# Split-weight buffers handed out block by block, and three of four block sums on VectorE instead of two

## The chip, the cores and the metric

The kernel runs on one core of one Trainium2 chip. The metric is the device time of one execution in microseconds (us); less is better. Times before come from three runs and one profiled execution.

## The reference, cut to what matters

One step of a streaming encoder with two layers for 640 rows (512 of a prompt, 8 x 16 of running streams), in fp32. Layer 0 is a convolution module, layer 1 an attention over a shared K and V; each is followed by a feed-forward network (FFN), and only these two networks are touched here:

```python
D_MODEL = 1024
FFN_HIDDEN = -(-8 * D_MODEL // (3 * 256)) * 256      # 2816

def swiglu_ffn(h, g, w_in, w_out):
    a, b = jnp.split(rms_norm(h, g) @ w_in, 2, axis=-1)
    return h + (jax.nn.silu(a) * b) @ w_out
...
    for l in range(DEPTH):
        ...
        h = swiglu_ffn(h, norm_ffn[l], w_ffn_in[l], w_ffn_out[l])
    return rms_norm(h, norm_final), jnp.stack(new_hist, axis=0), k, v
```

## The kernel before, in words

**Order of the program.** The convolution module runs first (to about 250 us of the span), then `ffn(0, ...)` (to about 690 us), the attention (to about 1060 us), `ffn(1, ...)` (to about 1505 us) and the last norm. Instructions are put in order at build time by a scheduler that runs a model of the engines' times; code under `tc.high_priority(offset=HP)` goes ahead of other code that is ready. On the chip each engine's queue then runs in that fixed order.

**A product in three passes.** A weight and an activation are each split into a rounded upper part (`hi`) and a rest (`lo`), and a product is hi x hi + lo x hi + hi x lo: three matmuls for each 128 rows of the contraction (`product`, line 374). The split of a weight is `put` (line 318): ScalarE (ACT) copies the source to `hi`, VectorE (DVE) subtracts it for `lo`. `cut` (line 322) does this for some columns of a pair of tiles.

**Seven products in place of eight.** The 640 columns of activations are two halves of 320 (`NH`), and the rows of the hidden layer are taken in pairs of 128. Most 2 x 2 products of blocks are formed with seven block products (a Strassen-like scheme): of a weight block with the quarters a11, a12, a21, a22 it needs a11, a12 and a22, and four sums. `w_seven` (line 352) loads a raw block (four quarters of 512 columns for `w_in`, 384 for `w_os`), forms the sums and cuts all seven. In order of the code:

- the SyncE (SP) queue loads a21 into `s1` and the whole block into `raw`;
- GpSimd (POOL) issues two adding DMAs from memory: a22 is added to `s1` (line 361), a11 to the quarter a21 of `raw` (line 362);
- one wide cut of a12 and a11 together (line 363), then DVE adds `s1` to a11 (line 364), and the cuts of that sum (XT2) and of `s1` (XT1);
- the cuts XT3 (of a21 + a11), XT4 (of a22) and X22 (of a12 plus the large sum, added by DVE on line 370).

The large pair `whi`, `wlo` (2048 columns, two buffers, `wbig`) takes the first four, the ring `shi`, `slo` (512 columns, three buffers, `wring`) the last three. `raw` has two buffers and `s1` two.

**Who uses a block when.** `seven` (line 460) runs the products of a `w_in` block in the order X11, X21, XT2, XT1, XT3, and hands the last two, XT4 and X22, to the next block, which runs them behind its own X11 and X21. A product of a `w_in` block has 12 matmuls, of a `w_os` block 9. For the output weights the order is written out in the string `QORD`: of each two characters the first names the product (5 is XT1, 1 X11, 2 X21, 6 XT2, 3 X22, 7 XT3, 4 XT4) and the second the pair of output rows; `a0` and `a1` are the products left over from the last `seven`.

**Counts.** A layer has three `w_in` blocks that go the plain way (`w_std`, eight products each), 19 that go through `w_seven`, and 12 of `w_os` (three chunks of four): 38 + 24 = 62 blocks of seven for both layers. The last four rows of hidden blocks go through plain products whose weights are split into `wbig` pairs at the end (line 602).

Of the kernel before, what the change touches and what calls it, by code (L numbers as in the profile page):

```python
# [9 lines left out]
F32R = mybir.dt.float32r  # L10
# [5 lines left out]
P = 128  # L16
# [41 lines left out]
X11, X21, XT2, XT1, XT3, XT4, X22 = range(7)  # L58
NCH, CW = 3, 6
HIX = {X11: 0, X21: 1, XT1: 2, XT2: 3, XT3: 4, X22: 5, XT4: 6}  # L60
QORD = "50 a0 10 a1 20 51 11 21 60 30 61 70 31 52 40 71 12 22 41 62 32 53 72 13 23 42 63 33"
BO = "a0 s0 a1 s1 b0 b1 t0 p0 c0 t1 c1"
BL = "a0 s0 a1 s1 t0 b0 b1 c0 t1 c1 p0"
SSQ1 = 'ppapappp'
# [10 lines left out]
def tile_trunk(ctx, tc, xT, vecs, hist, w_pw1, w_pw2, w_in0, w_out0, w_os0, w_in1, w_out1, w_os1,  # L75
               w_kq, w_v, w_o, rel, kc, vc, y_out, convp_out, convs_out, k_out, v_out):
    nc = tc.nc

    cst = ctx.enter_context(tc.tile_pool(name="cst", bufs=1))
    wp = ctx.enter_context(tc.tile_pool(name="wp", bufs=2))  # L80
# [11 lines left out]
    def nm(s):  # L92
        uid[0] += 1
        return f"{s}_{uid[0]}"
# [191 lines left out]
    def ffn(l, w_in, w_out, w_os, tail, hf):  # L286
        nonlocal w2, mm, tp

        def fpool(name, bufs, **kw):
            return hf.enter_context(tc.tile_pool(name=f"{name}{l}", bufs=bufs, reuse_waits="tile",  # L290
                                                 **kw))
# [13 lines left out]
        wx = fpool("wx", 2)  # L305
# [4 lines left out]
        sub, add, mult = ALU.subtract, ALU.add, ALU.mult  # L310

        def two(i, dt=F32R):
            return hpf.tile([P, 2, NH], dt, tag=f"d{i}", name=nm("hid"))
# [4 lines left out]
        def put(hi, lo, src):  # L318
            nc.scalar.activation(out=hi, in_=src, func=AF.Copy)  # L319
            nc.vector.tensor_tensor(out=lo, in0=src, in1=hi.bitcast(F32), op=sub)  # L320

        def cut(w, o, src):
            c = slice(o, o + src.shape[-1])
            put(w[0][:, c], w[1][:, c], src)

        def wraw():
            return wp.tile([P, 2048], F32, tag="raw", name=nm("raw"))

        def wbig():
            return [wp.tile([P, 2048], F32R, tag="w" + t, name=nm("w" + t)) for t in ("hi", "lo")]  # L330

        def wring():
            return [wx.tile([P, 512], F32R, tag="s" + x, name=nm("s" + x), bufs=3)
                    for x in ("hi", "lo")]

        def w_std(src, small):
            raw = wraw()
            if small:
                ws = [(wring(), 0) for _ in range(3)]
                ws.append(([two(i).rearrange("p a n -> p (a n)") for i in (12, 13)], 0))  # L340
            else:
                w = wbig()
                ws = [(w, 512 * i) for i in range(4)]
            for i in range(0, 2048, 1024):
                nc.sync.dma_start(raw[:, i:i + 1024], src[:, i:i + 1024])
                with tc.high_priority(offset=HP):
                    n = 512 if small else 1024
                    for j in range(i, i + 1024, n):
                        cut(*ws[j // 512], raw[:, j:j + n])
            return ws[1], ws[0], ws[2], ws[3]  # L350

        def w_seven(src, out=False):
            n = src.shape[-1] // 4
            raw, w = wraw(), wbig()
            s1 = wx.tile([P, 512], F32, tag="s1", name=nm("s1"))[:, :n]
            nc.sync.dma_start(s1, src[:, 2 * n:3 * n])
            nc.sync.dma_start(raw[:, :4 * n], src)
            a12, a11, a21, a22 = (raw[:, n * i:n * i + n] for i in range(4))
            ws = {X11: (w, n), X21: (w, 0), XT2: (w, 2 * n), XT1: (w, 3 * n)}
            with tc.high_priority(offset=HP):  # L360
                nc.gpsimd.dma_start(s1, src[:, 3 * n:4 * n], accum_op=add)
                nc.gpsimd.dma_start(a21, src[:, n:2 * n], accum_op=add)
                cut(w, 0, raw[:, :2 * n])
                nc.vector.tensor_tensor(out=a11, in0=s1, in1=a11, op=add)  # L364
                cut(w, 2 * n, a11)
                cut(w, 3 * n, s1)
                for x in (X22, XT3, XT4) if out else (XT3, XT4, X22):
                    ws[x] = (wring(), 0)
                    if x == X22:
                        nc.vector.tensor_tensor(out=a12, in0=a12, in1=a11, op=add)  # L370
                    cut(*ws[x], {X22: a12, XT3: a21, XT4: a22}[x])
            return ws

        def product(pt, w, xs, first, o=0):
# [85 lines left out]
        def seven(src, sink, before):  # L460
            ws = w_seven(src)
            pa, pb = mmt()[:, :NH], mmt()[:, :NH]
            xproduct(pa, ws[X11], X11, True)
            t1 = keep("t1", pa)
            before(0)
            xproduct(pb, ws[X21], X21, True)
            plus(t1, pb)
            silu(t1, t1)
            before(1)
            xproduct(pa, ws[XT2], XT2, False)  # L470
            t2 = keep("t2", pa)
            pe = mmt()[:, :NH]
            xproduct(pe, ws[XT1], XT1, True)
            xproduct(pa, ws[XT3], XT3, False)
            t3 = keep("t3", pa)
            plus(t3, pe)

            def after(i):
                if i == 0:
                    xproduct(pa, ws[XT4], XT4, False)  # L480
                    sink(0, t1, pa)
                else:
                    xproduct(pe, ws[X22], X22, False)
                    plus(t2, pe)
                    silu(t2, t2)
                    sink(1, t2, t3)

            return after

        def out_chunk(c, HH, HL, after):  # L490
            ws, pts = {}, {}
            prod = {5: ("e", XT1, True, 1, 1), 1: ("a", X11, True, 0, 0),
                    2: ("b", X21, True, 0, 0), 6: ("a", XT2, False, 1, 0),
                    3: ("e", X22, False, 1, 0), 7: ("a", XT3, False, 1, 1),
                    4: ("a", XT4, False, 0, 1)}

            def go(i, u):
                if u not in ws:
                    o = (4 * c + u) * 12 * P
                    ws[u] = w_seven(w_os[:, o:o + 12 * P], True)  # L500
                b, x, first, half, row = prod[i]
                if first:
                    pts[b, u] = mmt()[:, :NH]
                pt = pts[b, u]
                product(pt, ws[u][x], list(zip(HH[x], HL[x])), first)
                hv = h[:, 2 * u + row, half * NH:half * NH + NH]
                with tc.high_priority(offset=HP):
                    nc.vector.tensor_tensor(out=hv, in0=hv, in1=pt, op=sub if row else add)  # L508

            for t in QORD.split():  # L510
                if t[0] == "a":
                    after(int(t[1]))
                else:
                    go(int(t[0]), int(t[1]))
            return lambda i: go((7, 4)[i], 3)
# [42 lines left out]
        for jj in range(NSTD):  # L558
            wstd.append(w_std(w_in[jj], jj == 0))
            std(wstd[jj], 0, sinks[jj])  # L560
            if jj == 0:
                with tc.high_priority(offset=HP):
                    stats(1)
                    xnorm(x12, 1, 0)
                    xput(XT4, x12)
                    xnorm(x22, 1, 4)
                    xput(X22, x22)
# [32 lines left out]
        after(1)  # L600
        done = []
        for m0 in (0, 4):
            raw, w = wraw(), wbig()
            nc.sync.dma_start(raw.rearrange("p (m c) -> p m c", m=4),
                              w_out[m0:m0 + 4].rearrange("m p c -> p m c"))
            with tc.high_priority(offset=HP):
                for o in range(0, 2048, 1024):
                    cut(w, o, raw[:, o:o + 1024])
            done += [(m0 + i, [(w[0][:, b:b + P], w[1][:, b:b + P])
                               for b in range(512 * i, 512 * i + 512, P)]) for i in range(4)]  # L610
        for g0, n in tail:
            for m, w in done:
# [3 lines left out]
                with tc.high_priority(offset=HP):  # L616
                    nc.vector.tensor_tensor(out=h[:, m, g0:g0 + n], in0=pt[:, :n],
                                            in1=h[:, m, g0:g0 + n], op=add)
# [243 lines left out]
    early.close()  # L862
    hf = ExitStack()
    ffn(0, w_in0, w_out0, w_os0, GR, hf)
    hf.close()
    gr[:] = GR
# [286 lines left out]
    for p in range(NP):  # L1153
# [8 lines left out]
        for op in (BL if p == NP - 1 else BO).split():  # L1162
            i = int(op[1])
# [20 lines left out]
    for g0, n in ((0, NH), (NH, NH)):  # L1184
        for m in range(KT):
# [3 lines left out]
                            for wh, wl in wos for k in range(2)],  # L1189
                [(oT[4 + k][0][:, g0:g0 + n], oT[4 + k][1][:, g0:g0 + n]) for k in range(4)])  # L1190
            nc.vector.tensor_tensor(out=h[:, m, g0:g0 + n], in0=pt[:, :n], in1=h[:, m, g0:g0 + n],
                                    op=ALU.add)
    at.close()
    early.close()

    hf = ExitStack()
    ffn(1, w_in1, w_out1, w_os1, ((256, 384), (0, 256)), hf)
    tw[0] = 384
    sqt[:] = "sq", "acc", 1
# [8 lines left out]
    for g in (1, 0):  # L1208
        g0, n = GR[g]
        for k in range(KT):  # L1210
            if k < FP[g]:
                nc.vector.scalar_tensor_tensor(out=hp(g, k), in0=hp(g, k), scalar=col(V_NFIN, k),
                                               in1=bcs[g], op0=ALU.mult, op1=ALU.mult)
# [100 lines left out]
```

## Time and profile before

| | |
|---|---|
| time, median of three runs | 1539.4 us (1534.5 to 3146.81) |
| time of the profiled execution | 1537.75 us |
| its span | 1535.9 us |
| mean granted TensorE clock | 0.983 |
| busy: TensorE (PE) / its weight loads (PEld) | 95% / 90% |
| busy: DVE / ACT / POOL | 70% / 48% / 22% |
| from HBM, written | 193.82 MB, 11.61 MB |

Busy shares are of the span. A matmul is shown with its whole length, and consecutive ones overlap. In rows of groups stand the line of the kernel, engine, operation, output from inputs, shape and count, then the busy time, the mean of one in ns, and the engine's idle time just before with what ended it. In rows of waits stand the total in us, the count and the longest. Rows of instructions begin with start and length in us; in brackets is the engine's idle time before it.

### The profile page before, as it was taken

The numbers are of one execution on the slowest core, as the hardware profiler recorded it, in microseconds if no ns is written. First come the engines' busy times: TensorE is split into PE (matmuls) and PEld (weight loads), VectorE is DVE, ScalarE is ACT, GpSimd is POOL, SyncE is SP. The second block draws the span as 40 slices with busy tenths as digits, with TensorE's granted clock in tenths as the row PEclk, the third lists the DMA queues.
The fourth block names the chain that finished last, engine by engine and source line by source line (L and its number), as shares of the span: only waits on it lengthen the run. The fifth ranks groups of instructions, "written<-read, shape, count | busy, mean of one in ns | idle before, by whom it ended". The sixth has DMA issues, their size and how long they took to land.

```text
span 1535.9 us, 28172 instructions
## 1 busy us (share of the span) xinstructions
PE 1456.9 (95%) x10974; PEld 1376.3 (90%) x10974; DVE 1082.2 (70%) x2357; ACT 739.7 (48%) x1555; POOL 337.9 (22%) x374
## 2 busy tenths in 40 slices
PE   5999899999999999999999999978999999999995
PEld 5998689999999999999887888957999999999994
DVE  5789346788688677676676666654788678688664
ACT  3666246453453553455564453542554454454442
POOL 5789222011111111113221121111001111111101
PEclk9999899999999999999999999998999999999997
DMA  7267414146655655534565455541235665665521
GB/s 235 63 188 181 100 56 137 42 97 146 155 136 142 157 134 127 152 117 146 189 190 189 139 173 192 172 154 42 69 72 136 152 149 127 156 147 134 146 90 69
DMA packets 79941, 207.25 MB, mean 135 GB/s; under 512 B 12992, under 2 KB 37312, under 8 KB 71360
## 3 DMA queue, kind: packets, MB, share of 16 engines
q1 hardware_dynamic: 61664, 175.78, 35.6%
q0 software_dynamic: 17856, 29.37, 12.5%
q8 instruction: 86, 1.41, 0.4%
q14 instruction: 47, 0.39, 0.1%
q10 hardware_dynamic: 288, 0.31, 0.1%
HBM read 193.82 MB, written 11.61 MB: 134 GB/s over the span
## 4 chain that ended last, share of the span: by engine, by line
PE 46%; DMA 22%; DVE 17%; ACT 6%; POOL 5%; issue 3%; SPq 0%; POOLq 0%; DVEq 0%; ACTq 0%
PE mm L379 13%; DMA raw<-in_w_in 9%; PE mm L167 8%; PE mm L168 7%; PE mm L169 7%; DMA raw<-in_w_os 6%; DVE wlo L320 4%; DMA s<-in_w_in 4%; POOL ca L726 4%; ACT whi L319 4%; DVE slo L320 3%; PE mm L764 2%; DVE raw L364 2%; DVE h L508 1%; PE w L203 1%
## 5 line engine op out<-in xcount | busy, mean ns | idle before, releaser
L379 PE MATMUL mm<-XH,whi 128*128 128x320 f32 x736 | 223.3, 312 | 8.9 <-ACT whi L319 8.9
L379 PE MATMUL mm<-XH,wlo 128*128 128x320 f32 x736 | 227.8, 311 | 1.3 <-DVE wlo L320 1.3
L379 PE MATMUL mm<-XL,whi 128*128 128x320 f32 x736 | 226.4, 310 | 0.0
L320 DVE TENSOR_TENSOR wlo<-raw,whi 128x1024 fp32r<-128x1024 f32 (+3 forms) x140 | 127.5, 917 | 124.1 <-ACT whi L319 123.9
L167 PE MATMUL mm<-xh,whi 128*128 128x320 f32 (+2 forms) x640 | 200.8, 316 | 4.3 <-ACT xh L156 2.6
L168 PE MATMUL mm<-xh,wlo 128*128 128x320 f32 (+2 forms) x640 | 200.0, 313 | 0.6 <-DVE wlo L151 0.6
L319 ACT ACTIVATE whi<-raw 128x1024 fp32r<-128x1024 f32 (+3 forms) x140 | 113.0, 814 | 178.5 <-DMA raw<-in_w_in 75.9
L169 PE MATMUL mm<-xl,whi 128*128 128x320 f32 (+2 forms) x640 | 197.1, 312 | 0.0
L379 PE MATMUL mm<-XH,shi 128*128 128x320 f32 x504 | 156.1, 310 | 3.7 <-ACT t L388 3.2
L379 PE MATMUL mm<-XH,slo 128*128 128x320 f32 x504 | 155.0, 308 | 0.0
L379 PE MATMUL mm<-XL,shi 128*128 128x320 f32 x504 | 154.4, 308 | 0.1
L379 PEld LDWEIGHTS mm<-XH,whi 128*128 128x128 f32 x736 | 137.1, 189 | 11.1 <-ACT whi L319 11.0
L319 ACT ACTIVATE shi<-raw 128x512 fp32r<-128x512 f32 (+1 forms) x192 | 110.9, 582 | 69.0 <-PE mm L379 61.4
L379 PEld LDWEIGHTS mm<-XH,wlo 128*128 128x128 f32 x736 | 138.8, 189 | 2.6 <-DVE wlo L320 2.4
L379 PEld LDWEIGHTS mm<-XL,whi 128*128 128x128 f32 x736 | 138.5, 189 | 0.0
L379 PE MATMUL mm<-hid,whi 128*128 128x320 f32 x576 | 135.2, 309 | 0.6 <-ACT whi L319 0.6
L320 DVE TENSOR_TENSOR slo<-raw,shi 128x512 fp32r<-128x512 f32 (+1 forms) x192 | 121.2, 635 | 11.3 <-ACT shi L319 10.8
L167 PEld LDWEIGHTS mm<-xh,whi 128*128 128x128 f32 x640 | 121.4, 190 | 7.8 <-ACT xh L156 3.1
L168 PEld LDWEIGHTS mm<-xh,wlo 128*128 128x128 f32 x640 | 121.7, 190 | 1.2 <-DVE wlo L151 0.8
L169 PEld LDWEIGHTS mm<-xl,whi 128*128 128x128 f32 x640 | 120.8, 190 | 1.2 <-issue 1.0
L379 PE MATMUL mm<-hid,shi 128*128 128x320 f32 x432 | 106.7, 312 | 2.9 <-ACT shi L319 1.6
L379 PEld LDWEIGHTS mm<-XH,shi 128*128 128x128 f32 x504 | 94.5, 187 | 6.2 <-ACT t L388 5.6
(228 smaller groups left out, 3503.3 us busy)
## 6 DMA issues: line engine op xcount, KB each, us to landing
raw<-in_w_in SPq DMA_DIRECT2D x38, 1024.0 KB
raw<-in_w_os SPq DMA_DIRECT2D x24, 768.0 KB
cache<-in_ck SPq DMA_DIRECT2D x32, 512.0 KB
cache<-in_cv SPq DMA_DIRECT2D x32, 512.0 KB
raw<-in_w_pw SPq DMA_DIRECT2D x12, 1024.0 KB
s<-in_w_in SPq DMA_DIRECT2D x38, 256.0 KB
s<-in_w_in POOLq DMA_DIRECT2D x38, 256.0 KB, 4.7
raw<-in_w_in POOLq DMA_DIRECT2D x38, 256.0 KB, 4.2
```

Of the source, the lines that this page charges most:

```text
L167: nc.tensor.matmul(ps, wh, xh, start=(i == 0), stop=False)
L168: nc.tensor.matmul(ps, wl, xh, start=False, stop=False)
L169: nc.tensor.matmul(ps, wh, xl, start=False, stop=(i == last))
L203: nc.tensor.matmul(st[:, 512 + t * w + k:513 + t * w + k], s[:, a:a + P], onec, start=True, stop=True)
L319: nc.scalar.activation(out=hi, in_=src, func=AF.Copy)
L320: nc.vector.tensor_tensor(out=lo, in0=src, in1=hi.bitcast(F32), op=sub)
L364: nc.vector.tensor_tensor(out=a11, in0=s1, in1=a11, op=add)
L379: nc.tensor.matmul(pt, wt, v, start=(first and k == i == 0), stop=(k == len(xs) - 1 and i == 2), skip_group_check=True)
L508: nc.vector.tensor_tensor(out=hv, in0=hv, in1=pt, op=sub if row else add)
L726: nc.gpsimd.tensor_tensor(out=acc, in0=acc, in1=pr, op=ALU.add)
L764: nc.tensor.matmul(pt[32 * q:32 * q + 32, 0:n], w4[0:r, 4 * tg + q, :], mv, start=(tg == 0), stop=(tg == 7))
```

## The change

All seven cuts of a block now take places from one round of eleven: the three pairs of the former ring, each with a tag of its own, and four quarters of each of two large pairs that are allocated once for the layer. A counter deals them out in the order in which the code asks, which for a `w_in` block is the order of use of its products and for a `w_os` block the order of `QORD` (XT1 first). The wide cut becomes two of one quarter each. The adding DMA of line 362 is gone: DVE forms a21 + a11 ahead of the large sum. `w_std` takes four or three places from the same round; the last weights of the layer go straight into the two large pairs. In `QORD`, X21 of the second pair of rows (21) comes two places later, and 61 with 70 and 52 with 40 change places.

```diff
-QORD = "50 a0 10 a1 20 51 11 21 60 30 61 70 31 52 40 71 12 22 41 62 32 53 72 13 23 42 63 33"
+QORD = "50 a0 10 a1 20 51 11 60 30 21 70 61 31 40 52 71 12 22 41 62 32 53 72 13 23 42 63 33"
...
-        def wbig():
-            return [wp.tile([P, 2048], F32R, tag="w" + t, name=nm("w" + t)) for t in ("hi", "lo")]
-
-        def wring():
-            return [wx.tile([P, 512], F32R, tag="s" + x, name=nm("s" + x), bufs=3)
-                    for x in ("hi", "lo")]
+        wbig = [[wp.tile([P, 2048], F32R, tag="w" + t, name=nm("w" + t)) for t in ("hi", "lo")]
+                for _ in range(2)]
+        slots = [(wx.tile([P, 512], F32R, tag=f"shi{i}", name=nm("shi"), bufs=1),
+                  wx.tile([P, 512], F32R, tag=f"slo{i}", name=nm("slo"), bufs=1), 0)
+                 for i in range(3)]
+        slots += [(hi, lo, o) for hi, lo in wbig for o in range(0, 2048, 512)]
+        turn = [0]
+
+        def slot():
+            turn[0] += 1
+            hi, lo, o = slots[(turn[0] - 1) % len(slots)]
+            return (hi, lo), o
 
         def w_std(src, small):
             raw = wraw()
             if small:
-                ws = [(wring(), 0) for _ in range(3)]
+                ws = [slot() for _ in range(3)]
                 ws.append(([two(i).rearrange("p a n -> p (a n)") for i in (12, 13)], 0))
             else:
-                w = wbig()
-                ws = [(w, 512 * i) for i in range(4)]
+                ws = [slot() for _ in range(4)]
...
         def w_seven(src, out=False):
             n = src.shape[-1] // 4
-            raw, w = wraw(), wbig()
+            raw, ws = wraw(), {}
             s1 = wx.tile([P, 512], F32, tag="s1", name=nm("s1"))[:, :n]
             nc.sync.dma_start(s1, src[:, 2 * n:3 * n])
             nc.sync.dma_start(raw[:, :4 * n], src)
             a12, a11, a21, a22 = (raw[:, n * i:n * i + n] for i in range(4))
-            ws = {X11: (w, n), X21: (w, 0), XT2: (w, 2 * n), XT1: (w, 3 * n)}
             with tc.high_priority(offset=HP):
                 nc.gpsimd.dma_start(s1, src[:, 3 * n:4 * n], accum_op=add)
-                nc.gpsimd.dma_start(a21, src[:, n:2 * n], accum_op=add)
-                cut(w, 0, raw[:, :2 * n])
-                nc.vector.tensor_tensor(out=a11, in0=s1, in1=a11, op=add)
-                cut(w, 2 * n, a11)
-                cut(w, 3 * n, s1)
-                for x in (X22, XT3, XT4) if out else (XT3, XT4, X22):
-                    ws[x] = (wring(), 0)
-                    if x == X22:
+                for x in ((XT1, X11, X21, XT2, X22, XT3, XT4) if out else
+                          (X11, X21, XT2, XT1, XT3, XT4, X22)):
+                    if x == XT2:
+                        nc.vector.tensor_tensor(out=a21, in0=a11, in1=a21, op=add)
+                        nc.vector.tensor_tensor(out=a11, in0=s1, in1=a11, op=add)
+                    elif x == X22:
                         nc.vector.tensor_tensor(out=a12, in0=a12, in1=a11, op=add)
-                    cut(*ws[x], {X22: a12, XT3: a21, XT4: a22}[x])
+                    ws[x] = slot()
+                    cut(*ws[x], {XT1: s1, X11: a11, X21: a12, XT2: a11, X22: a12, XT3: a21,
+                                 XT4: a22}[x])
             return ws
...
         for m0 in (0, 4):
-            raw, w = wraw(), wbig()
+            raw, w = wraw(), wbig[m0 // 4]
```

## The prediction

> **What bounds the kernel now.** I read the page first, then the windows of the two feed-forward layers, which are the only code that the change touches, then who TensorE waits for there, and last the queues behind those waits.
>
> ```profile
> span 1535.9 us, 28172 instructions
> PE 1456.9 (95%) x10974; PEld 1376.3 (90%) x10974; DVE 1082.2 (70%) x2357; ACT 739.7 (48%) x1555; POOL 337.9 (22%) x374
> ```
>
> TensorE (PE) is busy for 95% of the span, so a change in the helpers of the weight blocks can win back only idle time of PE. How much of that lies in the two layers is in their windows (PE, PEld, DVE, ACT, POOL busy, then the granted clock, the DMA share and GB/s):
>
> ```profile
> 250.00:680.00 430.00, 420.57 (x2853) 415.92 (x2853) 326.01 (x647) 212.22 (x417) 53.17 (x61) 1.00 0.52 134
> 1060.00:1505.00 445.00, 435.22 (x2932) 429.51 (x2931) 328.42 (x653) 208.59 (x412) 53.44 (x62) 1.00 0.48 119
> 300.00:325.00 25.00, 25.00 (x173) 25.00 (x172) 22.48 (x48) 13.77 (x30) 1.72 (x2) 1.00 0.30 79
> L379 PE MATMUL mm<-XH,wlo 128*128 128x320 f32 x736 | 227.8, 311 | 1.3 <-DVE wlo L320 1.3
> ```
>
> PE is idle for 430 - 420.57 + 445 - 435.22 = 19.2 us in both layers together. A stretch without a gap holds 173 matmuls in 25 us, one every 0.145 us, though one is shown as 0.311 us long: two overlap. So each wait costs its idle time and some 0.311 - 0.145 = 0.166 us of lost overlap. What the matmuls of the layers (line 379) wait for (total us, times, longest):
>
> ```profile
> PE mm L379 <- ACT whi L319: 9.5, 9, 1.9
> PE mm L379 <- ACT t L388: 3.2, 8, 0.7
> PE mm L379 <- ACT shi L319: 1.6, 5, 0.4
> PE mm L379 <- DVE wlo L320: 1.3, 2, 0.8
> PE mm L379 <- DVE h L508: 1.1, 4, 0.4
> ```
>
> The three rows of split weights (whi, shi, wlo) are 12.4 us in 16 waits, with the lost overlap 12.4 + 16 x 0.166 = 15.1 us. The row of t is 3.2 + 8 x 0.166 = 4.5 us, that of h 1.8 us. All five together are 21.4 us: that is the ceiling of what this change can reach, but for the clock.
>
> ```profile
> 384.00:388.00 4.00, 2.19 (x8) 2.19 (x9) 2.21 (x4) 1.69 (x2) 0.86 (x1) 0.74 1.04 333
> 388.00:392.00 4.00, 4.00 (x25) 4.00 (x25) 3.36 (x6) 2.27 (x4) 0.86 (x1) 0.84 0.76 158
> ```
>
> Around the longest wait of the first layer the granted clock was 0.74 and 0.84 for 4 us each: 4 x 0.26 + 4 x 0.16 = 1.7 us more. (Other windows of the layers show 1.00.)
>
> **Why the weights are late.** The raw block of a weight has two buffers. SP's issues of raw blocks, and ACT at the same time:
>
> ```profile
> 1213.30 0.33 SPq L357 DMA_DIRECT2D raw<-in_w_in  x1
> 1227.34 0.33 SPq L357 DMA_DIRECT2D raw<-in_w_in  x1
> 1237.65 0.33 SPq L357 DMA_DIRECT2D raw<-in_w_in  x1
> 1250.01 0.33 SPq L357 DMA_DIRECT2D raw<-in_w_in  x1
> ...
> 1220.79 1.06 ACT L319 ACTIVATE whi<-raw 128x1024 fp32r<-128x1024 f32 x1 [4.09 <-DMA raw<-in_w_in]
> 1232.69 1.06 ACT L319 ACTIVATE whi<-raw 128x1024 fp32r<-128x1024 f32 x1 [2.47 <-DMA raw<-in_w_in]
> 1233.66 0.61 ACT L319 ACTIVATE shi<-raw 128x512 fp32r<-128x512 f32 x1
> 1234.90 0.62 ACT L319 ACTIVATE shi<-raw 128x512 fp32r<-128x512 f32 x1
> 1243.33 1.06 ACT L319 ACTIVATE whi<-raw 128x1024 fp32r<-128x1024 f32 x1 [1.27 <-DMA raw<-in_w_in]
> ```
>
> A buffer is taken again 24.4 us (1213.30 to 1237.65) and 22.7 us (1227.34 to 1250.01) later. PE's need is 7 products of 12 matmuls, 7 x 12 x 0.145 = 12.2 us a block, 24.4 us for two. So the hold of a raw buffer is as long as PE's two blocks, and any transfer that lands late reaches PE. A transfer takes 7.5, 5.4 and 5.7 us from issue to the first cut; the spread of 2.1 us is about the longest wait of PE, 1.9 us. And the loop feeds itself: the last two cuts of block B (1233.66 and 1234.90, into the small ring) stand on ACT behind the wide cut of the next block C, which waited 2.47 us for its transfer; only after them is B's buffer free (1237.65). They stand so late because the ring has three places: a cut there waits for the product of the same kind of the block before, and two of these run only after the next block's first products. Sums of ACT's waits over the whole span:
>
> ```profile
> ACT whi L319 <- DMA raw<-in_w_in: 75.9, 31, 4.8
> ACT shi L319 <- PE mm L379: 61.4, 41, 4.0
> ACT whi L319 <- DMA raw<-in_w_os: 45.3, 22, 3.3
> ACT whi L319 <- DMA s<-in_w_in: 19.6, 16, 2.2
> ```
>
> **The change, part by part.** *Slots.* Eleven places (three of the ring, eight quarters of the two large pairs) go round in the order of use. The last cut of a block, X22, then takes the place of XT2 of the block before, whose product runs six products ahead of the one it waited for. ACT can make a block's seven cuts in one run, ahead of the next block's wide wait, and the raw buffer comes free at landing plus ten DVE instructions (seven lower halves, three sums). These are issued 0.60 us apart at 512 columns:
>
> ```profile
> 1237.53 0.69 DVE L370 TENSOR_TENSOR raw<-raw 128x512 f32<-128x512 f32 x1
> 1238.13 0.49 DVE L415 SCALAR_TENSOR_TENSOR B<-t,t 128x320 f32<-128x320 f32 x1
> 1221.88 1.23 DVE L320 TENSOR_TENSOR wlo<-raw,whi 128x1024 fp32r<-128x1024 f32 x1 [6.29 <-ACT whi L319]
> 1223.02 0.48 DVE L415 SCALAR_TENSOR_TENSOR B<-t,mm 128x320 f32<-128x320 f32 x1
> ```
>
> Ten of them are 6 us; with the other work between them at three quarters load I estimate 10 us, against 1237.65 - 1220.79 = 16.9 us now. The hold falls from 24 to about 17 us, and the 7 us gained are over three times the spread of the transfers. So the whi, wlo and shi waits go: 15.1 us (bounds 0 and 15.1; I take all, since the slack is that much larger than the lateness). Of the t waits, where an evacuation stands on ACT behind a cut that waits, I take half, 2.2 us (0 to 4.5). With the long waits the dip of the clock goes: 1.7 us (0 to 1.7).
>
> On that last term the Trainium skill, TensorE: Matmul & The Clock Gate, Part 1, has another rule: the array falls to half rate only after an idle window of about 3.4 us. The longest wait here is 1.9 us and the granted clock dipped all the same, so the trace does not agree; by the rule the term would be 0 and the time 1.7 us longer.
>
> *The second sum by VectorE instead of an adding DMA.* Each of 62 blocks (38 of 512 columns, 24 of 384) gets one more sum:
>
> ```profile
> L364 DVE TENSOR_TENSOR raw<-s,raw 128x512 f32<-128x512 f32 x38 | 26.1, 686 | 0.2
> L364 DVE TENSOR_TENSOR raw<-s,raw 128x384 f32<-128x384 f32 x24 | 13.3, 552 | 0.0
> L362 POOL DMA_DIRECT2D raw<-in_w_in x38 | 33.2, 874 | 224.0 <-DMA raw<-in_w_in 150.3 <-DVE wlo L320 21.2 <-DVE hid L320 17.9
> raw<-in_w_in POOLq DMA_DIRECT2D x38, 256.0 KB, 4.2
> ```
>
> At start-to-start (0.09 us under the duration) that is 38 x 0.60 + 24 x 0.46 = 33.8 us. Splitting the wide cut in two costs DVE 2 x 0.60 - 1.14 = 0.06 us a block, 3.7 us over 62. Together 37.5 us on DVE, beside PE's products. Gone are 62 issues on POOL of 0.87 us, which stood between the issues that sum s1, and 38 x 256 + 24 x 192 KB of transfers; none of that was on PE's path except through the raw wait already counted: 0.
>
> What hides the 37.5 us is DVE's idle time in the blocks:
>
> ```profile
> 1190.00:1310.00 120.00, 116.03 (x780) 114.06 (x779) 90.92 (x179) 57.89 (x114) 17.41 (x20) 1.00 0.58 141
> 1310.00:1425.00 115.00, 112.65 (x761) 111.43 (x761) 88.66 (x174) 56.21 (x112) 18.32 (x21) 1.00 0.59 145
> ```
>
> DVE is busy 179.6 of 235 us, 76%. These stretches hold some 12 wide and 8 narrow blocks, so 12 x 0.66 + 8 x 0.52 = 12.1 us come on top: 82%. It fits, but the queue is in order, and a longer burst makes an evacuation or a lower half late. Bounds: 0 and the whole 37.5 us. Today's waits of PE for DVE (wlo, 1.3 + 2 x 0.166 = 1.6 us, and h, 1.8 us) are 3.4 us; I let that much come anew, since load grows by a twelfth.
>
> *First block in two halves.* X11 alone is cut in two instructions of 0.6 us instead of 1.06 and 1.23 us, so the first product can start a little over 1 us after landing, not 2.3. With the slack above it is no longer on the path: 0, but a cover if some transfer is still late.
>
> *QORD and the large pairs held through the layer.* The order of output products moves X21 of the second rows behind two others, swaps two pairs and changes no count: 0. At the end of each layer the last weights go into the same pairs; the last block's XT2 to XT4 stand in the first of them, so its first wide cut (1.06 + 1.23 = 2.3 us) must wait for XT1, with three products (3 x 12 x 0.145 = 5.2 us) as cover. Bounds 0 to 2.3 us for each layer; I take 1 each, 2 us.
>
> **The sum.** 15.1 + 2.2 + 1.7 - 3.4 - 2.0 = 13.6 us less. The profiled execution took 1537.75 us (its span 1535.9), 1.65 us under the median of the runs shown, 1539.4, and inside their common spread from 1534.5; I keep 1537.75 as the base: 1524 us, 0.9% less. The likeliest case's own range is from the ceiling (1537.75 - 21.4 - 1.7 = 1514.6) to no change.
>
> **The rivals.** *1. The wait moves to the adding DMA that is left.* s1 still needs a load, an issue on POOL and 4.7 us or so to land, and ACT already waited 19.6 us for it in 16 places. In an output block the cut of s1 now comes first.
>
> ```profile
> s<-in_w_os POOLq DMA_DIRECT2D x24, 192.0 KB, 4.8
> L319 ACT ACTIVATE whi<-s 128x384 fp32r<-128x384 f32 x24 | 11.7, 511 | 0.8 <-DMA s<-in_w_os 0.8
> ```
>
> If each of the 16 places still holds its 1.2 us, PE's gain is eaten: 1537 us, no change. Against it: the s1 of output blocks were in time (0.8 us of idle in all), and the second issue that stood ahead on POOL is gone.
>
> *2. Slower: the s1 cut blocks ACT.* If that leading cut comes before its sum has landed, everything behind it on ACT (evacuations, the other six cuts) waits. From the point where the sum lands later than the slot comes free, each of 24 output blocks loses up to 4.8 us less the cover of one product of 9 matmuls (1.3 us), 3.5 us at most; at half of that the loss is 42 us: 1537.75 + 42 - 6 (half of the gain) = 1574 us. For it: ACT is in order and blocks on just such a cut in the rows above. Against it: 0.8 us over 24.
>
> *3. DVE becomes the bound.* If all 37.5 us fall on PE's path: 1537.75 + 37.5 - 13 = 1562 us. For it: single windows already show 22.48 of 25 us. Against it: 82% on the average of two blocks.
>
> The Trainium skill, VectorE: DVE Perf Modes, Terms, says that the next operation cannot issue until the pipe of the last has emptied. The rows above show a start 0.60 us after that of an instruction of 0.69 us, so the trace does not bear it out as a full serial cost. By the rule, 38 x 0.686 + 24 x 0.552 + 62 x 0.15 = 48.6 us would come on top, and this rival's time would be 1573 us.
>
> *4. The slots do not act one by one.* If a write into one quarter waited for readers of the whole pair, the look-ahead would shrink to less than now, and each of 62 blocks could lose the 2.3 us of a first cut, 143 us: some 1680 us. Against it: products read one part of whi now while other parts of it are still to be written.
>
> *5. More than the five rows.* All of them and the clock gone, the other 2.5 us of the layers' idle time too (19.2 - 16.7), and a shift as between the runs shown (1539.4 - 1534.5 = 4.9 us) on top: 1514.6 - 2.5 - 4.9 = 1507 us. For it: an earlier first block helps every wait behind it. Against it: no stage outside the layers changes.
>
> **How the numbers follow.** Main case 0.57; rival 1 0.16; rival 2 0.09; rival 3 0.07; rival 4 0.03; rival 5 0.08. A measurement of this kernel tells about 2% (31 us) from no change, so faster by more means under 1508.6, slower over 1570.2. Faster: rival 5, 0.08. Slower: rivals 2 and 4 and a little of 3, 0.13. The rest, 0.79, within 2%. The range reaches from rival 5's side of the ceiling, 1508, over no change to short of rival 3, 1558, which leaves out rivals 2 and 4, most of 3 and half of 5, about 0.2.
>
> **What would show it.** Right: the whi row of PE's waits under 3 us; ACT's wait for raw transfers under a third of 121 us; issues of raw blocks earlier against their use; line 362 gone from POOL; DVE's busy time up by some 37 us, PE's idle time in the layers near 8 us, and all other windows as before. Wrong: whi<-s waits of ACT growing (rivals 1 and 2), PE waiting for wlo, slo or h (rival 3), or cuts waiting for products of their own block (rival 4).

## The result, and the profile after

The changed kernel takes 1526.97 us (median of 8 runs, from 1519.0), the kernel before 1542.97 us (median of 8, from 1534.5): a ratio of 0.9901, 95% interval 0.9874 to 0.9927, about 15 us. A second comparison gave 0.9891 (0.9853 to 0.9929). By the bound of 2% this is no change; the interval is clear of 1. Medians stand here because single disturbed runs of both kernels lay far above the rest, and the ratios leave those out.

The head of the page after:

```profile
span 1528.9 us, 28150 instructions
PE 1456.1 (95%) x10974; PEld 1378.4 (90%) x10974; DVE 1120.0 (73%) x2481; ACT 746.7 (49%) x1617; POOL 281.8 (18%) x312
```

VectorE has 37.8 us more to do (1082.2 before), POOL 62 instructions fewer. The windows of the two feed-forward layers, with the columns as before:

```profile
250.00:680.00 430.00, 424.84 (x2906) 421.48 (x2905) 351.36 (x720) 220.12 (x459) 31.36 (x36) 1.00 0.42 118
1050.00:1497.00 447.00, 440.63 (x2983) 437.44 (x2982) 348.66 (x718) 214.78 (x448) 30.56 (x35) 1.00 0.37 104
```

PE is idle there for 5.2 + 6.4 = 11.6 us, where it was 19.2 us, and the same matmuls need less time: from the first product of each layer to its last output matmul (the last that reads `hid`; in layer 0 it ends at 699.46 us before and at 695.09 us after) the traces have 863.1 us for both layers before and 849.7 us after (865.3 and 849.7 in second profiles of the two). The PE waits of the layers, now on line 383:

```profile
PE mm L383 <- DVE t L397: 3.0, 2, 2.1
PE mm L383 <- ACT whi L319: 2.9, 5, 0.6
PE mm L383 <- DVE XL L320: 1.3, 2, 0.7
PE mm L383 <- ACT shi L319: 1.1, 2, 0.6
PE mm L383 <- ACT t L392: 0.6, 2, 0.3
PE mm L383 <- DVE h L512: 0.3, 1, 0.3
```

Split weights (whi, shi) cost 4.0 us of idle where they cost 12.4 us, and t on ACT 0.6 where it cost 3.2. What is new is t on VectorE, 3.0 us in two waits. Ahead of the longer one, 2.1 us, VectorE's queue stood 5.3 us on the adding DMA that is left. That is in the waits of ACT and DVE:

```profile
ACT whi L319 <- PE mm L383: 105.0, 106, 4.2
ACT whi L319 <- DMA raw<-in_w_in: 24.9, 5, 8.1
ACT shi L319 <- DMA raw<-in_w_in: 12.7, 3, 7.9
ACT whi L319 <- DMA raw<-in_w_os: 4.9, 5, 1.2
DVE raw L369 <- DMA raw<-in_w_in: 23.6, 19, 4.0
DVE raw L370 <- DMA s<-in_w_in: 14.3, 5, 5.3
```

ACT waited 121 us for raw transfers before and 42.5 us now. Its 105 us of waits for products are those of an engine that is ahead: it waits for a place to come free. A part of the wait for transfers has moved to VectorE, whose first sum (line 369) is now what meets a raw block that has just landed.

How far ahead a raw block is asked for can be worked out from SP's issues and the matmuls counted in the program's order (PE's order may differ from it by a product, 1.7 us): the median of 31 blocks was 10.2 us in layer 0 and 9.2 us in layer 1 before, and is 21.9 and 21.6 us now.

Outside the layers the profiled executions of the changed kernel took longer. The stretch between the layers is attention, whose code is the same. Here it is from the last output matmul of layer 0 to the first product of layer 1, and below it its last part (before, then after):

```profile
699.46:1081.90 382.44, 365.71 (x3098) 314.87 (x3096) 242.63 (x701) 177.36 (x467) 72.11 (x119) 0.98 0.49 159
1000.00:1060.00 60.00, 47.65 (x399) 34.18 (x398) 29.01 (x79) 22.04 (x52) 8.61 (x13) 0.89 0.41 120
...
695.09:1081.03 385.94, 368.15 (x3097) 316.95 (x3096) 242.85 (x703) 177.56 (x467) 70.97 (x119) 0.97 0.48 158
1000.00:1060.00 60.00, 47.43 (x383) 33.75 (x382) 27.45 (x76) 21.36 (x51) 6.82 (x8) 0.83 0.38 115
```

It went from 382.4 us to 385.9 us, and both second profiles agree (382.3 and 386.1). It is not another order of PE's work: in the first profiles of the two kernels all 3096 matmuls of the stretch come in the same order. PE's idle time is nearly the same (16.7 and 17.8 us); the granted clock differs. In the 60 us shown it is 0.89 and 0.83, which is 60 x 0.06 = 3.6 us. Over the whole stretch the traces have 13.7 and 10.2 us at half clock in the two profiles of before, 20.5 and 17.1 us in those of after. Why there is more of it was not settled. The timed runs show no such loss: their mean clock is 0.983 before (18 runs) and 0.982 after (7 runs).

So the layers won 13 to 16 us, and attention took 3.6 us back in these profiles. In the profiled executions 6.8 us are left (1537.75 to 1530.94 us), in the medians of timed runs 15 to 16: the profiled execution of before was among the shorter of its runs, that of after among the longer. The stage ahead of the layers varies too: it took 266.1 us in the first profile of before, 268.5 us in the second, and 268.8 and 267.6 us in those of after.

### The profile page after: what moved, and what is told of

It is laid out like the page before. It is cut to its first block, busy times and chain, and to the rows that moved or that the text cites. A ratio compares the mean times of both kernels' runs of the same rounds, so it can differ in the third digit from the quotient of the medians.

```text
span 1528.9 us, 28150 instructions
## 1 busy us (share of the span) xinstructions
PE 1456.1 (95%) x10974; PEld 1378.4 (90%) x10974; DVE 1120.0 (73%) x2481; ACT 746.7 (49%) x1617; POOL 281.8 (18%) x312
## 3 DMA queue, kind: packets, MB, share of 16 engines
q1 hardware_dynamic: 61664, 175.78, 35.7%
## 4 chain that ended last, share of the span: by engine, by line
PE 77%; DVE 8%; POOL 5%; DMA 5%; ACT 3%; issue 2%; SPq 0%; POOLq 0%; DVEq 0%; ACTq 0%
PE mm L383 44%; PE mm L167 7%; PE mm L168 7%; PE mm L169 7%; POOL ca L730 4%; PE mm L768 2%; DMA raw<-in_w_in 1%; PE w L1105 1%; PE w L203 1%; PE am L1090 1%; DVE wlo L320 1%; DMA cache<-in_ck 1%; PE am L1073 1%; PE am L1136 1%; DMA s<-in_w_in 1%
## 5 line engine op out<-in xcount | busy, mean ns | idle before, releaser
L383 PE MATMUL mm<-XH,whi 128*128 128x320 f32 x896 | 275.8, 310 | 4.5 <-DVE t L397 3.0
L383 PE MATMUL mm<-XH,wlo 128*128 128x320 f32 x896 | 276.5, 310 | 0.0
L383 PE MATMUL mm<-XL,whi 128*128 128x320 f32 x896 | 273.8, 309 | 0.0
L319 ACT ACTIVATE whi<-raw 128x512 fp32r<-128x512 f32 (+2 forms) x280 | 166.3, 612 | 156.7 <-PE mm L383 90.5
L320 DVE TENSOR_TENSOR wlo<-raw,whi 128x512 fp32r<-128x512 f32 (+2 forms) x280 | 183.6, 670 | 14.1 <-ACT whi L319 12.7
L383 PEld LDWEIGHTS mm<-hid,whi 128*128 128x128 f32 x732 | 124.9, 188 | 4.0 <-ACT whi L319 3.4
L383 PE MATMUL mm<-hid,wlo 128*128 128x320 f32 x366 | 112.5, 308 | 0.0
L383 PE MATMUL mm<-XL,shi 128*128 128x320 f32 x344 | 105.4, 308 | 1.3 <-DVE XL L320 1.3
L383 PE MATMUL mm<-XH,shi 128*128 128x320 f32 x344 | 106.0, 308 | 0.4 <-ACT XH L319 0.4
L383 PE MATMUL mm<-XH,slo 128*128 128x320 f32 x344 | 106.0, 308 | 0.1
```

Source lines behind the costliest of these rows:

```text
L383: nc.tensor.matmul(pt, wt, v, start=(first and k == i == 0), stop=(k == len(xs) - 1 and i == 2), skip_group_check=True)
```

## The experiments

The theories at the start: A, the places handed out in the order of use free the raw buffers early and give the gain; B, the gain is from taking an adding DMA off the transfers and POOL's queue; C, VectorE is short of time.

**One part alone: the sum.**

```diff
-                nc.gpsimd.dma_start(a21, src[:, n:2 * n], accum_op=add)
                 cut(w, 0, raw[:, :2 * n])
+                nc.vector.tensor_tensor(out=a21, in0=a11, in1=a21, op=add)
                 nc.vector.tensor_tensor(out=a11, in0=s1, in1=a11, op=add)
```

> The kernel before with one edit: the second sum (a21 + a11) is formed by VectorE and its adding DMA is gone; buffers, wide cut and order of products stay. Theory A (the gain comes from handing the places out in the order of use, which frees the raw buffers earlier): same as before within 4 us, PE's waits for whi still 8 us or more. Theory B (the gain comes from taking an adding DMA off the transfers and off POOL's queue): most of the gain is already here, 10 us or more faster than before. Theory C (VectorE is short of time): 5 us or more slower than before.

Measured: 1.0031 of before (1.0011 to 1.0050). Without the adding DMA, and with its old buffers, the kernel is a little slower: 6 us by the medians, 5 us by the ratio, about the bound that theory C gave. Theory B alone falls. The layers took 863.9 us, as before (863.1). PE's waits for results of ACT fell from 14.3 to 8.6 us, those for results of VectorE rose from 2.4 us (4.2 us in the second profile of before) to 9.3 us:

```profile
PE mm L379 <- ACT whi L319: 7.4, 8, 2.6
PE mm L379 <- DVE slo L320: 3.9, 4, 1.7
PE mm L379 <- DVE wlo L320: 2.8, 4, 0.7
...
ACT shi L319 <- PE mm L379: 91.5, 72, 3.4
...
DVE raw L363 <- DMA raw<-in_w_in: 54.2, 30, 5.6
```

VectorE's queue now stands on the landing of raw blocks (line 363), where it had no such wait before. The cuts into the ring still wait for products (91.5 us, 61.4 before). And ACT had next to nothing to win: in the kernel before, only two of its waits in front of a cut, 1.9 us together, ended with the landing of an adding DMA of line 362 (the cut starts within 0.12 us of it).

**The other part alone: the places.**

```diff
                 nc.gpsimd.dma_start(s1, src[:, 3 * n:4 * n], accum_op=add)
+                nc.gpsimd.dma_start(a21, src[:, n:2 * n], accum_op=add)
...
                     if x == XT2:
-                        nc.vector.tensor_tensor(out=a21, in0=a11, in1=a21, op=add)
```

> The changed kernel with one edit: the second sum goes back to the adding DMA; the places, the halved first cut and the new order of products stay. Theory A: 10 to 16 us faster than before, like the change. Theory B: within 4 us of before. Theory C: faster than the change by some us, since 34 us of VectorE work are gone.

Measured: 1.0000 of before (0.9977 to 1.0023). Theory A alone falls too, though its mechanism is there: raw blocks are asked for 22.3 us ahead (median of both layers), as in the changed kernel. So neither part gives anything by itself. Where the lead went is in four long waits of PE (2.3, 1.5, 3.7 and 3.9 us), with 13.7 us at half clock beside three of them. This is the longest (POOL, then ACT, then PE):

```profile
1331.42 0.86 POOL L366 DMA_DIRECT2D raw<-in_w_in  x1 [10.83 <-DVE h L512]
1337.93 0.88 POOL L366 DMA_DIRECT2D raw<-in_w_in  x1 [4.24 <-DMA raw<-in_w_in]
...
1339.45 0.63 ACT L319 ACTIVATE whi<-raw 128x512 fp32r<-128x512 f32 x1 [8.75 <-DMA raw<-in_w_in]
1340.50 0.42 ACT L392 ACTIVATE t<-mm 128x320 f32<-128x320 f32 x1
...
1340.97 0.64 PE L383 MATMUL mm<-XH,whi 128*128 128x320 f32 x1 [3.86 <-ACT t L392]
```

ACT stood for 8.75 us on a cut of a raw block. The next raw block had landed by 1337.93, where it let POOL go on, so what ended ACT's wait 1.5 us later was the adding DMA issued at 1331.42; the trace has its landing at 1339.42, 8.0 us after the issue. Behind the cut stood the evacuation of a product (line 392), and PE waited 3.86 us for it. Two more of the four waits are of this kind (the DMAs took 8.5 and 7.9 us). In the fourth, 3.7 us, VectorE's queue stood 7.84 us on the other sum, s1, whose DMA took 9.3 us. From here theory D: both parts are needed, because with places in the order of use the cut of a21 + a11 stands among the other cuts of its block in ACT's queue (here the build put it ahead of five of them), and waits there for a DMA that can only be issued after the raw block has landed.

**Fewer places.**

```diff
-            hi, lo, o = slots[(turn[0] - 1) % len(slots)]
+            hi, lo, o = slots[turn[0] - 1 if turn[0] < 4 else 3 + (turn[0] - 4) % 8]
```

> The changed kernel with eight places in the round instead of eleven (the three pairs of the former ring serve only the first block of a layer). The last cut of a block then waits for XT4 of the block before, which runs behind the next block's first product, much as in the kernel before. Theory A: most of the gain is lost, 1537 to 1545 us, and the raw buffers are held as long as before (about 24 us). Theory B or a gain from the halved cut alone: the gain stays, within 4 us of the change.

Measured: 1.0231 (1.0202 to 1.0260), 1577 us. This doesn't answer its question. In the order of the program an output block is cut while four products of the block before are still to come, so it needs 4 + 7 = 11 places. With eight, its cuts overwrite places that are still to be read: late products are formed with weights of the next block, the output is wrong, and these products come behind the next block's cuts. By the code, eleven is the least that this order of products allows; nine and ten were not tried.

**No adding DMA.**

```diff
-            nc.sync.dma_start(s1, src[:, 2 * n:3 * n])
...
-                nc.gpsimd.dma_start(s1, src[:, 3 * n:4 * n], accum_op=add)
+                nc.vector.tensor_tensor(out=s1, in0=a21, in1=a22, op=add)
```

> The changed kernel with the last adding DMA gone too: VectorE forms s1 = a21 + a22 from the raw block, so s1 needs neither a load nor an issue on POOL; VectorE gets 34 us more. If PE's remaining waits come from the late s1 (VectorE stood 5.3 us on it before the longest wait of PE, 2.1 us): 2 to 5 us faster than the change. If VectorE is now near its limit (some 88% in the blocks): 3 to 15 us slower than the change.

Measured: 0.9880 of before (0.9845 to 0.9914), 1523.77 us, some 3 us faster than the changed kernel, though the two intervals overlap. In the trace the layers are 844.6 us, 5.1 us shorter, and no PE wait for t on VectorE is left: the long waits of the changed kernel came from s1. VectorE has more to do here than in any kernel so far (76% of the span), so theory C doesn't hold for it.

**Traffic without a wait.**

```diff
+        spare = wx.tile([P, 512], F32, tag="spare", name=nm("spare"), bufs=1)
+        nc.gpsimd.memset(spare, 0.0)
...
                 nc.gpsimd.dma_start(s1, src[:, 3 * n:4 * n], accum_op=add)
+                nc.gpsimd.dma_start(spare[:, :n], src[:, n:2 * n], accum_op=add)
```

> The changed kernel with a second adding DMA for each block of seven, of the same size as the one removed, into a spare tile that nobody reads and that waits for no raw block. It adds the traffic and the POOL issues back, but no wait of a cut. The first runs showed neither part alone to help (the sum alone 1.0031, the places alone 1.0000 of before). Theory D (both are needed because, with places in the order of use, the cut of a21 + a11 stands on ACT in the middle of the block and waits there for a DMA that is issued only after the raw block has landed): time as the changed kernel, within 4 us. Theory B2 (the traffic of the adding DMA and its place in POOL's queue are the price): 8 us or more slower than the changed kernel, near 1540 us.

Measured: 1.0512 (1.0465 to 1.0560), 1620.67 us: slower, as theory B2 has it, but by far more than the 1540 us that it named. It is two single waits of PE, 35.7 us in layer 0 and 37.2 us in layer 1, and this is what the second waited for (POOL, then ACT):

```profile
1206.43 0.88 POOL L368 DMA_DIRECT2D spare<-in_w_os  x1 [3.24 <-DMA spare<-in_w_os]
1210.47 0.88 POOL L368 DMA_DIRECT2D spare<-in_w_in  x1 [3.15 <-DMA spare<-in_w_os]
1211.07 1.16 POOL L367 DMA_DIRECT2D s<-in_w_in  x1
...
1224.97 1.14 POOL L367 DMA_DIRECT2D s<-in_w_os  x1
...
1229.97 0.52 ACT L319 ACTIVATE whi<-s 128x384 fp32r<-128x384 f32 x1 [42.45 <-DMA s<-in_w_os]
```

The spare DMAs wait for nothing but each other, so the order put a run of them early on POOL's queue, one every 4 to 5 us for most, and the sums of s1 stood behind the run: the one that ACT waited for was issued at 1224.97. Without the two waits the layers are 928.8 - 72.9 = 855.9 us, 6.2 us over the changed kernel. So the traffic and the issues cost about that much at the most in this run, and the experiment shows what theory B had right: the place in POOL's queue can cost more than the transfer.

**The waiting cut moved to the end.**

```diff
-                for x in ((XT1, X11, X21, XT2, X22, XT3, XT4) if out else
-                          (X11, X21, XT2, XT1, XT3, XT4, X22)):
+                for x in ((XT1, X11, X21, XT2, X22, XT4, XT3) if out else
+                          (X11, X21, XT2, XT1, XT4, X22, XT3)):
```

This is an edit of the kernel with the places and the adding DMA.

> The kernel with places and the adding DMA (which ran as fast as before), with one edit: XT3, whose source waits for that DMA, is cut last of the seven and not fifth or sixth. Theory D: the wait moves behind the other cuts of its block and most of the gain appears, 1528 to 1536 us. Theory B2: no change, 1538 to 1545 us.

Measured: 0.9872 of before (0.9849 to 0.9895), 1522.56 us; the same kernel with XT3 in its old place had 1.0000. The adding DMA is back with all its traffic, and the whole gain is there. Theory D stands, theory B2 falls as the reason for the loss. The adding DMAs of 256 KB landed no sooner after their issue (medians of 4.5 us for a21 + a11 and 5.2 us for s1, against 4.3 and 4.8 us). But their landing ended a wait of ACT in front of a cut from `raw` 12 times, 13.4 us in all and 2.0 us at the longest, where with XT3 in its old place it was 22 times, 63.9 us and 8.75 us. The waits of PE that are left:

```profile
PE mm L383 <- ACT whi L319: 2.3, 4, 0.6
PE mm L383 <- ACT shi L319: 1.1, 2, 0.6
PE mm L383 <- DVE h L512: 0.6, 3, 0.3
```

The 4.6 us for t on VectorE and 4.4 us for t on ACT of the kernel with XT3 in the middle are gone or down to 0.5.

**VectorE's slack.**

```diff
                     if x == XT2:
+                        spare = wx.tile([P, 512], F32, tag="spare", name=nm("spare"), bufs=1)[:, :n]
+                        nc.vector.tensor_tensor(out=spare, in0=a11, in1=a12, op=add)
+                        nc.vector.tensor_tensor(out=spare, in0=a11, in1=a12, op=add)
```

> The changed kernel with two more sums of one block quarter on VectorE for each block of seven, into a spare tile that nobody reads: twice the work that the change put there, some 67 us more. If VectorE's idle time hides it (the prediction's view, load 82% going to 92%): under 8 us slower than the changed kernel. If VectorE is already what PE waits for: 20 us or more slower.

Measured: 0.9955 of before (0.9935 to 0.9975), 1533.98 us: 7 us over the changed kernel by the medians (8 us by the ratios) for some 62 us more of VectorE's busy time. The layers took 856.2 us, 6.5 us more. Of what is put on VectorE there, a little over a tenth reaches PE. For the 37.8 us of the change itself that is some 4 us, an estimate from these two runs that takes the cost to grow in proportion.

**Twelve places, no adding DMA.**

```diff
+        slots.append((wx.tile([P, 512], F32R, tag="shi3", name=nm("shi"), bufs=1),
+                      wx.tile([P, 512], F32R, tag="slo3", name=nm("slo"), bufs=1), 0))
...
-            s1 = wx.tile([P, 512], F32, tag="s1", name=nm("s1"))[:, :n]
+            s1 = wx.tile([P, 512], F32, tag="s1", name=nm("s1"), bufs=1)[:, :n]
```

> The kernel with no adding DMA at all, s1 with one buffer instead of two and a twelfth place from the room won. If the places still hold ACT up (its waits for products are 137 us there): 2 to 5 us faster than the kernel without adding DMA, 1519 us. If those waits cost PE nothing: the same, 1523 us within 3.

Measured: 0.9852 of before (0.9833 to 0.9872), 1518.8 us. It has the lowest median so far. Its interval and the first one of the changed kernel don't meet; it does meet the second one, and that of the kernel with eleven places and no adding DMA. Over 235 us of layer 1, where PE had been idle for 6.3 us before, it is not idle at all, with VectorE at 89%:

```profile
1190.00:1310.00 120.00, 120.00 (x821) 120.00 (x820) 108.32 (x219) 61.47 (x128) 0.00 (x0) 1.00 0.24 81
1310.00:1425.00 115.00, 115.00 (x786) 115.00 (x785) 101.70 (x206) 60.82 (x128) 0.00 (x0) 1.00 0.27 91
```

Its layers are 840.1 us, 4.5 us under those with eleven places, and ACT's waits for products with `whi` went from 136.9 to 106.9 us. Attention took 384.6 us, 1.2 us less than with eleven. So most of the 5 us between the two medians lies in the code that the twelfth place touches, as far as one profile of each can tell.

**The order of the cuts, without the places.**

```diff
-                for x in (X22, XT3, XT4) if out else (XT3, XT4, X22):
+                for x in (X22, XT4, XT3) if out else (XT4, X22, XT3):
```

> The kernel before with one edit: of the three cuts that go into the ring, XT3, whose source waits for the adding DMA, comes last (X22, XT4, XT3 for output blocks; XT4, X22, XT3 for the others). Theory D says that the places and the absence of a waiting cut in the middle of a block are both needed: here the ring still holds every cut for the product of its own kind, so the time stays at that of before, within 5 us, and raw blocks are still issued some 10 us ahead of use. If the order of the cuts alone were the cause: 10 us or more faster.

Measured: 1.0215 (1.0179 to 1.0250), 1577.97 us. The order alone is not the cause of the gain, as theory D has it, but the time didn't stay either: 34 us were lost.

```profile
PE mm L379 <- ACT whi L319: 32.1, 20, 3.8
...
ACT shi L319 <- PE mm L379: 102.6, 69, 4.0
```

In the order of products XT3 (7) comes before XT4 (4). The cut of XT4 waits in the ring for the XT4 product of the block before, and the cut that is needed first now stands behind it. Here an order of cuts against the order of use cost 34 us.

**One adding DMA, last, with twelve places.**

```diff
                 nc.vector.tensor_tensor(out=s1, in0=a21, in1=a22, op=add)
+                nc.gpsimd.dma_start(a21, src[:, n:2 * n], accum_op=add)
...
-                        nc.vector.tensor_tensor(out=a21, in0=a11, in1=a21, op=add)
```

XT3 is cut last, as in the sixth experiment.

> The fastest kernel so far (twelve places, s1 by VectorE without a load), with a21 + a11 back on the adding DMA and XT3 cut last: 34 us less on VectorE, 62 adding DMAs more. If VectorE's load still costs PE something there: 2 to 4 us faster, 1515 to 1517 us. If the DMA's wait costs as much as the sum: 1517 to 1522 us.

Measured: 0.9850 of before (0.9819 to 0.9881), 1521.02 us; not to be told from the kernel without adding DMA (0.9852). Here 42 waits of ACT in front of a cut from `raw` ended with the landing of an adding DMA, 60.6 us in all, about as much as in the kernel that gained nothing; but none was over 3.2 us. So in these two kernels it is the length of the single wait that tells, and not the sum. Beside it ran the two kernels unchanged.

> The kernel before, unchanged, for a second profile: in the profiled executions the stretch outside the two layers took 668 us before and 676 us in the changed kernel and in the kernel with the sum alone, whose code is the same there. If that is chance: some 676 us here too. If the change lengthens the other stages: 668 us again.

> The changed kernel, unchanged, beside the others on the same chip: 0.9901 of before, within 0.003.

Measured: the kernel before had a span of 1540.4 us, and attention of 382.3 us; the changed kernel 0.9891 (0.9853 to 0.9929), and attention of 386.1 us. The 668 and 676 us of the expectation let the layers end some matmuls too late. With the last output matmul as the end, the stretch outside the layers is 672.8 and 675.1 us in the two profiles of before, 679.2 and 678.1 us in those of after. So the longer attention is there in both profiles of the changed kernel, 3.6 us, with more time at half clock. It doesn't follow the change in the other kernels, whose attention is the same code: it took 381.4 us in the kernel with one adding DMA and twelve places (10.2 us at half clock) and 386.2 us in the kernel before with another order of cuts (23.9 us).

## Why the prediction was right or wrong, point by point

**The time.** 1524 us was forecast, 0.9% less; 1526.97 us and 0.9901 were measured. Against the 13.6 us of the sum stand 13.4 and 15.6 us in the layers of the two pairs of profiles. The terms below missed in both directions, so that the sum came so near is in part luck.

**What bounds the layers, and the ceiling.** Right. Waits of PE for weights were the larger part of what could be won, and even the best kernel won no more in the layers (863.1 to 840.1 us, 23.0) than the 21.4 + 1.7 us of the ceiling.

**Slots: whi, wlo and shi go, 15.1 us.** Two thirds of it came: 12.4 us of idle in 16 waits became 4.0 in 7, with the lost overlap 9.9 us. But the step put this down to the slots, and that failed: the slots by themselves gave 1.0000. Nor did the hold of a raw buffer fall from 24 to 17 us: a buffer is taken again after 23.6 and 22.9 us before (medians of the two layers) and after 23.0 and 22.5 us now, about the time that PE takes for two blocks. What grew is the lead over PE, from about 10 to about 22 us. What the step left out is that ACT's run of seven cuts contained one that waits for a DMA.

**"None of that was on PE's path except through the raw wait already counted: 0."** This is the step that was wrong for the adding DMA. Taken away with the slots in place, or moved to the end of the run, it is worth the whole gain; taken away with the ring, nothing. The two terms could not be priced one by one.

**t on ACT, half of 4.5 us.** More went: 3.2 us of idle in 8 waits became 0.6 in 2, with the lost overlap 3.6 us.

**The clock, 1.7 us.** The dip of layer 0 is gone and both windows show 1.00. But the second profile of the changed kernel has a dip of 3.4 us near its longest wait of 2.4 us, and the first one none at 2.1 us; the second profile of the kernel before has no dip in layer 0. So the term holds in some executions only.

**VectorE's load, 3.4 us for 37.5 us.** Right in size: 37.8 us more busy time, 83% in the two stretches that the prediction showed (82% forecast), and a cost of some 4 us by the experiment with two more sums. It fell on other rows than wlo and h: t on VectorE (3.0 us) and XL (1.3 us).

**The ends of the layers, 2.0 us.** Too high: no gap of PE beyond 0.3 us stands where the last weights are taken over.

**The order of products costs and gives nothing.** As a price this was not tried by itself. The code says more: with eleven places the old order would give the place of a product that hasn't run yet (40) to the third block, so the new order is a condition of the slots.

**Rival 1, the wait moves to s1.** Right as the next wait in line (14.3 us on VectorE, 3.0 us of PE), with a fifth of the price given for it: taking s1's DMA away gave some 3 us. **Rivals 2 to 5** did not come about; the blocking of ACT by a cut that waits for a sum, rival 2's mechanism, is what made the slots alone worth nothing, with the other sum.

**"All other windows as before."** Not in the profiles: attention was 3.6 us longer, with more time at half clock, though its matmuls and their order were the same. No run shows that the change is the cause. Two other signs were missed narrowly or by some: ACT's wait for raw transfers is 42.5 us where under a third of 121 us was named, and PE's idle time in the windows 11.6 us where 8 us were.

## What to carry to other kernels

An engine's queue is in order, so a buffer that comes free earlier is worth nothing while one instruction in the same run still waits for something late; look for every wait in the run, and put what waits longest last or take it away. Here a wait of 8 us in ACT's queue reached PE, and many waits of up to 3 us did not. Two edits that give nothing one by one can be worth 1% together, so try the pair before dropping either. Compare the stages that weren't touched too, from the same instruction to the same instruction: here one was 3.6 us longer in two profiles with the same work in the same order, and a lower granted clock.

## What the runs showed of the hardware that was not expected

An adding DMA of 256 KB landed 4 to 5 us after its issue in the median, but 8.0 us after it when a raw block and another sum were under way (1331.42 to 1339.42 in the kernel with the places alone). PE's granted clock followed the length of a wait only loosely: it dipped around a wait of 1.9 us in one execution and not around one of 2.1 us in another. And the same attention, with the same matmuls, had from 10.2 to 23.9 us at half clock from kernel to kernel.
